# Summing modulation vectors 1024 columns at a time in a two-layer conditioned decoder trunk

## The chip, the cores and the metric

The kernel runs on one core of one Trainium2 chip. The metric is the device time of one execution in microseconds (us), from launch to end on that core, as the median of several runs. Engines are named PE (TensorE matmul), PEld (TensorE weight load), DVE (VectorE), ACT (ScalarE), POOL (GpSimd) and SP (the queue that issues the DMAs); SPq marks an issue on it.

## What is computed

Two layers act on 256 tokens of width 1024, all in f32. A condition vector c of 1024 numbers makes six modulation vectors of 1024 a layer, which shift, scale and gate the two sub-layers:

```python
mod = jax.nn.silu(c) @ w_ada + b_ada                       # w_ada: 1024 x 6144 a layer, 25 MB
sh1, sc1, gt1, sh2, sc2, gt2 = jnp.split(mod, 6, axis=-1)
h = adaln(rms_norm(x, g_mix), sh1, sc1)                     # h * (1 + sc1) + sh1
q_a, k_a, v_a, q_b, k_b, v_b, gate_a, gate_b = jnp.split(h @ w_in, IN_OFFSETS, axis=-1)
q_a = rope(rms_norm(q_a, qn_swa), positions)                # and k_a, q_b, k_b
mixed = sigmoid(gate_a) * (swa_attention(...) @ w_o_swa) + sigmoid(gate_b) * (moba_attention(...) @ w_o_moba)
x = x + gt1 * (mixed @ w_out)
h = adaln(rms_norm(x, g_mlp), sh2, sc2)
x = x + gt2 * (square(relu(h @ w_up)) @ w_down)
```

`rope` turns each head's two halves: `x1*cos - x2*sin` and `x2*cos + x1*sin`. With the head gains g taken in, the kernel needs one table of `g*cos` and one of `g*sin` with the halves of g swapped and the first one negated.

## The kernel before

**Matmuls in three terms.** Each f32 weight is split into a rounded high part and the rest: ACT casts 1024 columns (L440), DVE subtracts (L446), and TensorE makes three matmuls of each product (`mm3`, L522 to L524, and `mm3f`, L527 to L529). The weights come as pieces of 1 MB (`Stream`), three raw buffers deep, and each piece is split in two halves into a handful of slots that come free as TensorE has used them.

**Stages.** `lead` is the first projection, with an order written out by hand (`tc.manual_schedule`). Then `mixing(0)` (the rest of the projections, head norm and rotation, attention in eight pairs of heads, 16 gate products, the two output products), `mlp(0)`, `mixing(1)` and `mlp(1)`. Between two sub-layers stands a boundary: DVE takes the four finished accumulators times the gate vector into x (`residual`: L640, then L641), ACT sums squares (L541), POOL raises to the power -1/2 (L545), DVE scales (L552), TensorE turns the rows (L570), and ACT and DVE apply scale and shift.

**The background.** While the stages run, `tick()` is called after every few matmuls. A tick may split one more weight half, takes one step of each chain in `bg` (head norm, rotation, attention), and one step of the first generator in `slow` (two while `pace` is 2, which holds in the last part of `mixing(0)`). The generators in `slow` are `ada_unit(u)`. What is left of them when an output product ends is run to its end there (L661).

**A unit before.** A unit is 512 columns of one of the six vectors. Row p*8+k of `w_ada` lies on partition p, so `silu(c) @ w_ada` is a sum of eight rows on each partition and then a sum over partitions. The unit loads four pieces of two rows by 512 columns (512 KB, L233; three buffers `araw`), takes eight DVE steps, one for each row (L256 for the first of a shift or scale, else L259), one a tick, into one of two `ada` buffers, and then has a tail. For a shift or scale the tail is four TensorE turns (L288), a DVE reduction (L294) and small DVE steps (L301, L304). For a gate it is a cast on ACT (L270), a subtraction on DVE (L271), two matmuls with ones (L274, L275), and a copy on ACT (L277). A gate's first step adds the bias row, which stands in row 0 of `bz` (memset on POOL at L150, loaded at L240). Steps to a unit: 13 for a gate, 11 for a shift or scale. Units 0 to 3 belong to the lead. `ADA_PLAN` gives units 4 to 9 to `mixing(0)`, 10 to 19 to `mlp(0)`, 20 and 21 to `mixing(1)`, 22 and 23 to `mlp(1)`.

**What sets the order.** Outside the lead a planner orders each engine's instructions with a list schedule: among those that its own costs show as ready, the one that stands first in the program is issued. So a later instruction can run early where an engine would be idle, and it holds the engine until it is done. At run time every engine, and SP's queue, keeps that order and waits at its head.

**Rotary tables.** `rope_gains` (called in the lead, L1036) scales the head gains by 8 and makes the swapped copy `gsw`; `rope_tables(l)` makes the tables of a layer in eight DVE steps (L383), in the lead for layer 0 (L1021).

Of the kernel before, what the change touches and what calls it, by code (L numbers as in the profile page):

```python
# [8 lines left out]
F32 = mybir.dt.float32  # L9
# [6 lines left out]
P = 128  # L16
S = 256
D = 1024
# [55 lines left out]
ADA_PLAN = (range(4, 10), range(10, 20), range(20, 22), range(22, 24))  # L74
# [4 lines left out]
def kernel(ctx: ExitStack, tc: tile.TileContext, io):  # L79
# [39 lines left out]
    gsw = const.tile([P, DEPTH, 4, HD], F32, name="gsw")  # L119
# [29 lines left out]
    bz = const.tile([P, 512], F32, name="bz")  # L149
# [47 lines left out]
    for l in range(DEPTH):  # L197

        if l == 0:
            ada_units += [(0, 0, q) for q in range(4)]  # L200
        for parts in (((2,), (4, 3), (5,)) if l == 0 else ((1, 0), (4, 3), (2,), (5,))):
            for half in range(2):
                for part in parts:
                    ada_units.append((l, part, half))
# [5 lines left out]
    def ada_load(i):  # L210

        u, q = divmod(i, 4)
# [3 lines left out]
        col = part * D + half * 512  # L216
# [10 lines left out]
        if u < 4:  # L227
            for k in range(2):
                nc.sync.dma_start(
                    ada_raw[i][:, k, :].rearrange("p (a c) -> p a c", a=2),  # L230
                    src[:, 2 * q + k, 0:2 * D].rearrange("p (a c) -> p a c", a=2)[:, :, half * 256:half * 256 + 256])
        else:
            nc.sync.dma_start(ada_raw[i], src[:, 2 * q:2 * q + 2, col:col + 512])  # L233

    def bias_row(u):

        if u < len(ada_units) and ada_units[u][1] % 3 == 2:
            l, part, half = ada_units[u]
            c0 = part * D + half * 512
            nc.sync.dma_start(bz[0:1, :], io["b_ada"][l:l + 1, c0:c0 + 512])  # L240

    def ada_unit(u):

        l, part, half = ada_units[u]
        sub, kind = divmod(part, 3)
        acc = work.tile([P, 512], F32, tag="ada", name=nm("ada"), bufs=2)
        for q in range(4):
            for a in range(ADA_BUFS if u > 3 else 0):
                ada_load(4 * u + q + a)
            raw = ada_raw[4 * u + q]  # L250
            if q == 2:
                bias_row(u + 1)
            for k in range(2):
                kk = 2 * q + k
                if kk == 0 and kind < 2:
                    nc.vector.tensor_scalar(out=acc, in0=raw[:, k, :], scalar1=cs[:, kk:kk + 1], scalar2=None,  # L256
                                            op0=ALU.mult)
                else:
                    nc.vector.scalar_tensor_tensor(  # L259
                        out=acc, in0=raw[:, k, :], scalar=cs[:, kk:kk + 1], in1=(bz if kk == 0 else acc),  # L260
                        op0=ALU.mult, op1=ALU.add)
                yield
        yield
        if kind == 2:
            ps = tmp_t()
            if half == 0:
                gt[l][sub] = state.tile([P, D], F32, tag="gt", name=nm("gt"), bufs=2)
            hi = ring(512, "ghi").bitcast(F32R)
            lo = ring(512, "glo").bitcast(F32R)
            nc.scalar.copy(hi, acc)  # L270
            nc.vector.tensor_tensor(out=lo, in0=acc, in1=hi.bitcast(F32), op=ALU.subtract)  # L271
            for _ in range(G_LAG):
                yield
            nc.tensor.matmul(ps, lhsT=ones_r, rhs=hi, start=True, stop=False)  # L274
            nc.tensor.matmul(ps, lhsT=ones_r, rhs=lo, start=False, stop=True)  # L275
            yield
            nc.scalar.activation(gt[l][sub][:, half * 512:(half + 1) * 512], ps, AF.Copy,  # L277
                                 scale=(0.5 if sub == 0 else 1.0))
        else:
            ps = ada_sums(acc)  # L280
            yield
            ada_columns(l, sub, half, ps, 4, (kind,))
# [84 lines left out]
    def rope_gains():  # L367

        r8 = float(HD) ** 0.5
        nc.vector.tensor_scalar(out=gsw[:, :, :, 0:HALF], in0=gqk[:, :, :, HALF:], scalar1=-r8, scalar2=None,  # L370
                                op0=ALU.mult)
        nc.vector.tensor_scalar(out=gsw[:, :, :, HALF:], in0=gqk[:, :, :, 0:HALF], scalar1=r8, scalar2=None,
                                op0=ALU.mult)
        nc.vector.tensor_scalar(out=gqk, in0=gqk, scalar1=r8, scalar2=None, op0=ALU.mult)

    def rope_tables(l):

        ct = state.tile([P, 4, NT, HD], F32, tag="ct", name=nm("ct"), bufs=1)
        st = state.tile([P, 4, NT, HD], F32, tag="st", name=nm("st"), bufs=1)
        for t in range(NT):  # L380
            for h in range(2):
                for (o, g, i) in ((ct, gqk, 1), (st, gsw, 0)):
                    nc.vector.tensor_tensor(  # L383
                        out=o[:, :, t, h * HALF:(h + 1) * HALF], in0=g[:, l, :, h * HALF:(h + 1) * HALF],
                        in1=sincos[:, i, t, :][:, None, :].to_broadcast([P, 4, HALF]), op=ALU.mult)
# [495 lines left out]
    def lead():  # L881
# [113 lines left out]
        for q in range(4):  # L995
# [39 lines left out]
            if q == 0:  # L1035
                rope_gains()  # L1036
                load_rest()
# [235 lines left out]
```

## Time and profile before

| | |
|---|---|
| device time, 3 runs | 757.29 us median, 754.62 to 758.05 |
| the profiled execution: device time, span | 755.65 us, 753.9 us |
| PE busy | 730.7 us (97%), 4713 matmuls |
| PEld busy | 645.3 us (86%) |
| DVE busy | 587.2 us (78%), 1090 instructions |
| ACT busy | 431.2 us (57%) |
| POOL busy | 32.0 us (4%) |
| DMA | 173.46 MB, 230 GB/s over the span |
| TensorE's granted clock | 1.000 in the mean, full in all 40 slices |

The profiled execution lies 1.75 us outside its span, and 1.64 us under the median. Matmuls overlap and their ends are modelled, so a busy PE can hide small gaps; where PE is shown idle, it waited.

### The profile page before, as it was taken

How to read it: one execution, taken by the hardware profiler on the slowest of the kernel's cores; microseconds unless marked ns; L12 is line 12 of the kernel's file. 1: busy time of each engine (PE TensorE's matmuls, PEld its weight loads, DVE VectorE, ACT ScalarE, POOL GpSimd, SP SyncE). 2: the span in 40 equal slices, each digit the busy share in tenths (PEclk: the TensorE clock that was granted, in tenths of full speed). 3: DMA queues.
4: the chain of work that ended last, by engine and by line, in shares of the span. 5: the costliest groups of instructions: out<-in, count | busy, mean ns of one | idle time of the engine just before them, and what ended most of it. 6: DMA issues, size and time to landing. Idle time of an engine off the chain costs nothing.

```text
span 753.9 us, 12320 instructions
## 1 busy us (share of the span) xinstructions
PE 730.7 (97%) x4713; PEld 645.3 (86%) x4713; DVE 587.2 (78%) x1090; ACT 431.2 (57%) x817; POOL 32.0 (4%) x24
## 2 busy tenths in 40 slices
PE   7999889999999999999999999999999999999997
PEld 6678778899778999989977888989988899999896
DVE  6598998999899988988789788987879745545542
ACT  6545579863466655455436357576447755555550
POOL 1003200000000000000000401000000000000000
PEclk9999999999999999999999999999999999999999
DMA  8996758877949999989882633844662865565501
GB/s 293 392 325 227 227 162 285 274 254 248 303 128 330 370 347 299 332 309 342 283 318 98 224 119 113 263 157 166 225 223 80 269 203 175 182 207 172 189 33 57
DMA packets 110538, 173.46 MB, mean 230 GB/s; under 512 B 4744, under 2 KB 68488, under 8 KB 110480
## 3 DMA queue, kind: packets, MB, share of 16 engines
q1 hardware_dynamic: 109744, 172.54, 67.9%
q8 instruction: 37, 0.61, 0.3%
q10 hardware_dynamic: 736, 0.15, 0.1%
q14 instruction: 21, 0.17, 0.1%
HBM read 171.62 MB, written 1.05 MB: 229 GB/s over the span
## 4 chain that ended last, share of the span: by engine, by line
PE 72%; DVE 13%; DMA 7%; ACT 3%; issue 2%; POOL 2%; SPq 0%; ACTq 0%; DVEq 0%; POOLq 0%
PE tmp L527 11%; PE acc L524 11%; PE acc L522 11%; PE acc L523 11%; PE tmp L528 10%; PE tmp L529 10%; DMA araw<-in_w_ada_dram 4%; DVE ada L259 2%; DVE w L446 2%; PE acc L984 2%; POOL rs L751 1%; ACT w L440 1%; PE tmp L870 1%; DMA wraw<-in_w_up_dram 1%; PE acc L810 1%
## 5 line engine op out<-in xcount | busy, mean ns | idle before, releaser
L446 DVE TENSOR_TENSOR w<-wraw,w 128x1024 fp32r<-128x1024 f32 x137 | 166.3, 1221 | 48.1 <-ACT w L440 46.8
L440 ACT CAST w<-wraw 128x1024 fp32r<-128x1024 f32 x150 | 155.9, 1048 | 78.9 <-PE acc L524 44.5
L527 PE MATMUL tmp<-hT_hi,w 128*128 128x256 f32 x480 | 140.1, 292 | 1.3 <-DVE alo L874 1.2
L529 PE MATMUL tmp<-hT_hi,w 128*128 128x256 f32 x480 | 135.9, 283 | 0.0
L528 PE MATMUL tmp<-hT_lo,w 128*128 128x256 f32 x480 | 135.7, 283 | 0.0
L259 DVE SCALAR_TENSOR_TENSOR ada<-araw,cs,ada 128x512 f32<-128x512 f32 x140 | 104.4, 746 | 3.2 <-DMA araw<-in_w_ada_dram 2.1
L527 PEld LDWEIGHTS tmp<-hT_hi,w 128*128 128x128 f32 x480 | 91.5, 191 | 8.2 <-issue 4.4
L528 PEld LDWEIGHTS tmp<-hT_lo,w 128*128 128x128 f32 x480 | 91.7, 191 | 0.7
L529 PEld LDWEIGHTS tmp<-hT_hi,w 128*128 128x128 f32 x480 | 91.6, 191 | 0.3 <-issue 0.3
L522 PE MATMUL acc<-w,uhi 128*128 128x512 f32 x192 | 75.4, 393 | 0.0
L523 PE MATMUL acc<-w,uhi 128*128 128x512 f32 x192 | 74.9, 390 | 0.0
L524 PE MATMUL acc<-w,ulo 128*128 128x512 f32 x192 | 74.9, 390 | 0.0
L1164 ACT ACTIVATE relu<-tmp 128x256 f32<-128x256 f32 x56 | 21.5, 384 | 68.8 <-PE tmp L529 68.8
L524 PEld LDWEIGHTS acc<-w,ulo 128*128 128x128 f32 x192 | 36.1, 188 | 7.6
L522 PEld LDWEIGHTS acc<-w,uhi 128*128 128x128 f32 x192 | 36.1, 188 | 6.9
L523 PEld LDWEIGHTS acc<-w,uhi 128*128 128x128 f32 x192 | 36.1, 188 | 6.8
L440 ACT CAST kv<-wraw 128x1024 fp32r<-128x1024 f32 x21 | 22.1, 1051 | 24.6 <-PE acc L524 19.8
L446 DVE TENSOR_TENSOR ahi<-wraw,ahi 128x1024 fp32r<-128x1024 f32 x18 | 22.0, 1222 | 15.0 <-ACT ahi L440 14.9
L446 DVE TENSOR_TENSOR kv<-wraw,kv 128x1024 fp32r<-128x1024 f32 x21 | 25.7, 1222 | 9.9 <-ACT kv L440 9.8
L446 DVE TENSOR_TENSOR qT<-wraw,qT 128x1024 fp32r<-128x1024 f32 x21 | 25.6, 1220 | 8.3 <-ACT qT L440 8.3
L527 PE MATMUL tmp<-hT_hi,alo 128*128 128x256 f32 x112 | 31.8, 284 | 0.0
L528 PE MATMUL tmp<-hT_lo,alo 128*128 128x256 f32 x112 | 31.7, 283 | 0.0
(248 smaller groups left out, 1744.8 us busy)
## 6 DMA issues: line engine op xcount, KB each, us to landing
araw<-in_w_ada_dram SPq DMA_DIRECT2D x80, 512.0 KB, 5.9
wraw<-in_w_up_dram SPq DMA_DIRECT2D x32, 1024.0 KB, 5.9
wraw<-in_w_down_dram SPq DMA_DIRECT2D x32, 1024.0 KB, 5.9
wraw<-in_w_in_dram SPq DMA_DIRECT2D x28, 1024.0 KB, 5.7
wraw<-in_w_out_dram SPq DMA_DIRECT2D x8, 1024.0 KB, 5.6
wraw<-in_w_in_dram SPq DMA_DIRECT2D x12, 512.0 KB, 7.1
wraw<-in_w_o_swa_dram SPq DMA_DIRECT2D x8, 512.0 KB, 3.3
wraw<-in_w_o_moba_dram SPq DMA_DIRECT2D x8, 512.0 KB, 5.1
```

The costliest lines, as they stand in the source:

```text
L259: nc.vector.scalar_tensor_tensor(out=acc, in0=raw[:, k, :], scalar=cs[:, kk:kk + 1], in1=(bz if kk == 0 else acc), op0=ALU.mult, op1=ALU.add)
L440: nc.scalar.copy(hi, r)
L446: ins = nc.vector.tensor_tensor(out=lo, in0=r, in1=hi.bitcast(F32), op=ALU.subtract)
L522: nc.tensor.matmul(ps, lhsT=lh, rhs=rh, start=start, stop=False)
L523: nc.tensor.matmul(ps, lhsT=lh, rhs=rl, start=False, stop=False)
L524: nc.tensor.matmul(ps, lhsT=ll, rhs=rh, start=False, stop=stop)
L527: nc.tensor.matmul(ps, lhsT=wh, rhs=ah, start=start, stop=False)
L528: nc.tensor.matmul(ps, lhsT=wh, rhs=al, start=False, stop=False)
L529: nc.tensor.matmul(ps, lhsT=wl, rhs=ah, start=False, stop=stop)
L751: nc.gpsimd.tensor_tensor(out=rs, in0=ss, in1=mhalf[:, :NT * nh].rearrange("p (t h) -> p t h", h=nh), op=ALU.pow)
L984: T.matmul(ps[t], lhsT=left[:, 2 * q + k, t * P:(t + 1) * P], rhs=w[:, k, :], start=(first and k == 0), stop=(last and k == 1))
L1164: nc.scalar.activation(r, ps, AF.Relu)
```

## The change

Units 4 and up become whole vectors of 1024 columns, one row of `w_ada` a piece (still 512 KB). There are 10 of them in place of 20, with one `ada` buffer of 1024 in place of two of 512. The order of the vectors in layer 1 and the share of each stage stay as they were. Both halves of the tail run one after the other at the end of the unit. In `mixing(0)`'s shift and scale (units 5 and 6) the tail is the lead's `columns` (four matmuls with one column of ones, L335) instead of turns and a reduction. `rope_gains` and `gsw` go; `rope_tables` takes the unscaled gains with swapped halves and the factor 8 or -8 as a scalar.

```diff
-ADA_PLAN = (range(4, 10), range(10, 20), range(20, 22), range(22, 24))
+ADA_PLAN = (range(4, 7), range(7, 12), range(12, 13), range(13, 14))
...
-    bz = const.tile([P, 512], F32, name="bz")
+    bz = const.tile([P, D], F32, name="bz")
...
-            nc.sync.dma_start(ada_raw[i], src[:, 2 * q:2 * q + 2, col:col + 512])
+            nc.sync.dma_start(ada_raw[i].rearrange("p k c -> p (k c)"), src[:, q, part * D:(part + 1) * D])
...
-        acc = work.tile([P, 512], F32, tag="ada", name=nm("ada"), bufs=2)
+        acc = work.tile([P, D], F32, tag="ada", name=nm("ada"), bufs=1)
+        for k in range(KT):
+            for a in range(ADA_BUFS):
+                ada_load(16 + 8 * (u - 4) + k + a)
+            raw = ada_raw[16 + 8 * (u - 4) + k].rearrange("p k c -> p (k c)")
+            if k == 4:
+                bias_row(u + 1)
+            if k == 0 and kind < 2:
+                nc.vector.tensor_scalar(out=acc, in0=raw, scalar1=cs[:, k:k + 1], scalar2=None, op0=ALU.mult)
+            else:
+                nc.vector.scalar_tensor_tensor(out=acc, in0=raw, scalar=cs[:, k:k + 1], in1=(bz if k == 0 else acc),
+                                               op0=ALU.mult, op1=ALU.add)
+            yield
         yield
+        for half in range(2):
+            hs = slice(half * 512, (half + 1) * 512)
+            if kind == 2:
...
+                nc.scalar.copy(hi, acc[:, hs])
+                nc.vector.tensor_tensor(out=lo, in0=acc[:, hs], in1=hi.bitcast(F32), op=ALU.subtract)
+                for _ in range(G_LAG):
+                    yield
...
+            elif u in ADA_PLAN[0]:
+                ps = columns(acc[:, hs])
+                yield
+                ada_affine(l, sub, half, ps, 4, (kind,))
+            else:
+                ps = ada_sums(acc[:, hs])
+                yield
+                ada_columns(l, sub, half, ps, 4, (kind,))
...
-                for (o, g, i) in ((ct, gqk, 1), (st, gsw, 0)):
-                    nc.vector.tensor_tensor(
-                        out=o[:, :, t, h * HALF:(h + 1) * HALF], in0=g[:, l, :, h * HALF:(h + 1) * HALF],
+                for (o, i, f, gh) in ((ct, 1, r8, h), (st, 0, (r8 if h else -r8), 1 - h)):
+                    nc.vector.scalar_tensor_tensor(
+                        out=o[:, :, t, h * HALF:(h + 1) * HALF], in0=gqk[:, l, :, gh * HALF:(gh + 1) * HALF], scalar=f,
...
-                rope_gains()
                 load_rest()
```

## Rows read from the trace of the kernel before

**Rows 1.** Stretch: length; busy us (count) PE, PEld, DVE, ACT, POOL; clock, DMA, GB/s.
```profile
0.00:58.00 58.00, 51.77 (x279) 40.75 (x280) 41.16 (x92) 30.99 (x48) 2.81 (x10) 1.00 0.95 332
58.00:105.00 47.00, 40.75 (x263) 34.48 (x262) 42.03 (x94) 25.53 (x51) 12.48 (x4) 1.00 0.60 198
105.00:205.00 100.00, 98.80 (x740) 89.02 (x739) 92.03 (x205) 68.33 (x166) 0.00 (x0) 1.00 0.82 269
205.00:225.00 20.00, 17.53 (x96) 14.28 (x95) 19.44 (x42) 12.89 (x27) 1.61 (x2) 1.00 0.46 147
225.00:389.00 164.00, 164.00 (x1048) 149.23 (x1047) 143.45 (x201) 91.42 (x148) 0.00 (x0) 1.00 0.95 327
389.00:405.00 16.00, 13.37 (x66) 10.50 (x65) 14.17 (x32) 6.08 (x17) 1.47 (x2) 1.00 0.48 174
405.00:754.00 349.00, 344.50 (x2233) 306.99 (x2231) 234.97 (x431) 195.99 (x366) 13.61 (x6) 1.00 0.51 168
```

**Rows 2.** What PE waited for: us in total, times, longest.
```profile
PE tmp L570 <- DVE ln L552: 4.1, 2, 2.4
PE acc L984 <- ACT hT_hi L970: 3.2, 2, 2.0
```

**Rows 3.** The tile `ada`: instructions, ns min/median/max, first to last start in us, shapes.
```profile
L259 DVE SCALAR_TENSOR_TENSOR ada<-araw,cs,ada x140: 722/746/754, 75.5 to 499.1; 128x512 f32<-128x512 f32 x140
...
L256 DVE TENSOR_SCALAR ada<-araw,cs x12: 475/480/486, 119.0 to 350.2; 128x512 f32<-128x512 f32 x12
L259 DVE SCALAR_TENSOR_TENSOR ada<-araw,cs,bz x8: 740/746/752, 62.5 to 485.6; 128x512 f32<-128x512 f32 x8
```

**Rows 4.** DVE's groups by line: count, busy us, mean ns, idle before and its cause.
```profile
L446 DVE TENSOR_TENSOR w<-wraw,w 128x1024 fp32r<-128x1024 f32 x137 | 166.3, 1221 | 48.1 <-ACT w L440 46.8 <-PE tmp L793 0.7
...
L294 DVE TENSOR_REDUCE cols<-tmp 128x4 f32<-128x512 f32 x12 | 8.2, 686 | 2.5 <-PE tmp L288 2.5
```

**Rows 5.** Order of time, boundary before `mixing(1)`: start, us, instruction [idle before <- cause].
```profile
390.90 1.53 DVE L259 SCALAR_TENSOR_TENSOR ada<-araw,cs,ada 128x512 f32<-128x512 f32 x2
392.36 0.68 DVE L640 TENSOR_TENSOR res<-acc,gt 128x512 f32<-128x512 f32 x1
392.96 0.74 DVE L259 SCALAR_TENSOR_TENSOR ada<-araw,cs,ada 128x512 f32<-128x512 f32 x1
393.62 0.68 DVE L641 TENSOR_TENSOR x_sb<-x_sb,res 128x512 f32<-128x512 f32 x1
394.22 0.74 DVE L259 SCALAR_TENSOR_TENSOR ada<-araw,cs,ada 128x512 f32<-128x512 f32 x1
...
397.27 0.66 PE L570 MATMUL tmp<-cpack,ln 128*128 128x128 f32 x4 [2.43 <-DVE ln L552]
```

**Rows 6.** The lead's rotary tables and `columns`: ns min/median/max, first to last start.
```profile
L383 DVE TENSOR_TENSOR ct<-gqk,sincos x8: 262/283/286, 37.8 to 144.1; 128x128 f32<-128x128 f32 x8
...
L335 PE MATMUL tmp<-ones,arow x16: 169/250/250, 27.8 to 40.1; 128*128 128x1 f32 x16
```

**Rows 7.** Tile `ada` alone by stretch: busy us (count) PE, PEld, DVE, ACT.
```profile
58.00:105.00 47.00, 0.00 (x0) 0.00 (x0) 8.10 (x11) 0.64 (x1) 1.00 0.60 198
105.00:205.00 100.00, 2.39 (x16) 1.88 (x16) 29.69 (x42) 0.65 (x1) 1.00 0.82 269
...
225.00:389.00 164.00, 4.79 (x32) 3.83 (x32) 60.76 (x85) 1.22 (x2) 1.00 0.95 327
```

**Rows 8.** Order of time during `mixing(0)`'s rotation.
```profile
75.52 0.74 DVE L259 SCALAR_TENSOR_TENSOR ada<-araw,cs,ada 128x512 f32<-128x512 f32 x1
...
77.01 0.63 PE L793 MATMUL tmp<-cpack,ro 128*128 128x128 f32 x4 [1.09 <-DVE ro L785]
```

**Rows 9.** Order of time on DVE: unit 6's reduction, then unit 8's first step.
```profile
151.49 0.69 DVE L294 TENSOR_REDUCE cols<-tmp 128x4 f32<-128x512 f32 x1 [1.09 <-PE tmp L288]
152.09 0.48 DVE L256 TENSOR_SCALAR ada<-araw,cs 128x512 f32<-128x512 f32 x1
```

**Rows 10.** POOL's power at the boundaries: ns min/median/max, first to last start.
```profile
L545 POOL TENSOR_TENSOR lnr<-lnr,mhalf x6: 557/668/938, 206.0 to 570.5; 128x1 f32<-128x1 f32 x6
```

More of the change, by code (lines that the diff above doesn't have):

```diff
@@ L200 @@
             ada_units += [(0, 0, q) for q in range(4)]
[L201 to L204, printed above, removed]
+        ada_units += [(l, part, None) for part in ((2, 4, 3, 5) if l == 0 else (1, 0, 4, 3, 2, 5))]
     ada_raw = {}
@@ L232, in ada_load @@
         else:
-            nc.sync.dma_start(ada_raw[i], src[:, 2 * q:2 * q + 2, col:col + 512])
+            nc.sync.dma_start(ada_raw[i].rearrange("p k c -> p (k c)"), src[:, q, part * D:(part + 1) * D])
     def bias_row(u):
         if u < len(ada_units) and ada_units[u][1] % 3 == 2:
-            l, part, half = ada_units[u]
-            c0 = part * D + half * 512
-            nc.sync.dma_start(bz[0:1, :], io["b_ada"][l:l + 1, c0:c0 + 512])
+            l, part, _ = ada_units[u]
+            nc.sync.dma_start(bz[0:1, :], io["b_ada"][l:l + 1, part * D:(part + 1) * D])
@@ L242, in ada_unit @@
     def ada_unit(u):
-        l, part, half = ada_units[u]
+        l, part, _ = ada_units[u]
         sub, kind = divmod(part, 3)
-        acc = work.tile([P, 512], F32, tag="ada", name=nm("ada"), bufs=2)
[L247 to L251, printed above, removed]
-                bias_row(u + 1)
[L253 to L262, printed above, removed]
+        acc = work.tile([P, D], F32, tag="ada", name=nm("ada"), bufs=1)
@@ L263, in ada_unit @@
         yield
         if kind == 2:
[L265 to L272, printed above, removed]
-                yield
-            nc.tensor.matmul(ps, lhsT=ones_r, rhs=hi, start=True, stop=False)
@@ L275, in ada_unit @@
[L275 to L282, printed above, removed]
+            gt[l][sub] = state.tile([P, D], F32, tag="gt", name=nm("gt"), bufs=2)
+        for half in range(2):
+            hs = slice(half * 512, (half + 1) * 512)
+            if kind == 2:
+                ps = tmp_t()
+                hi = ring(512, "ghi").bitcast(F32R)
+                lo = ring(512, "glo").bitcast(F32R)
+                nc.scalar.copy(hi, acc[:, hs])
+                nc.vector.tensor_tensor(out=lo, in0=acc[:, hs], in1=hi.bitcast(F32), op=ALU.subtract)
+                for _ in range(G_LAG):
+                    yield
+                nc.tensor.matmul(ps, lhsT=ones_r, rhs=hi, start=True, stop=False)
+                nc.tensor.matmul(ps, lhsT=ones_r, rhs=lo, start=False, stop=True)
+                yield
+                nc.scalar.activation(gt[l][sub][:, hs], ps, AF.Copy, scale=(0.5 if sub == 0 else 1.0))
+            elif u in ADA_PLAN[0]:
[6 more added lines that the diff above has]
+                ada_columns(l, sub, half, ps, 4, (kind,))
@@ L365, in rope_sin @@
         nc.scalar.activation(pos_f, pos_f, AF.Tanh)
[L367 to L374, printed above, removed]
     def rope_tables(l):
@@ L379, in rope_tables @@
         st = state.tile([P, 4, NT, HD], F32, tag="st", name=nm("st"), bufs=1)
+        r8 = float(HD) ** 0.5
         for t in range(NT):
             for h in range(2):
-                for (o, g, i) in ((ct, gqk, 1), (st, gsw, 0)):
-                    nc.vector.tensor_tensor(
-                        out=o[:, :, t, h * HALF:(h + 1) * HALF], in0=g[:, l, :, h * HALF:(h + 1) * HALF],
-                        in1=sincos[:, i, t, :][:, None, :].to_broadcast([P, 4, HALF]), op=ALU.mult)
+                for (o, i, f, gh) in ((ct, 1, r8, h), (st, 0, (r8 if h else -r8), 1 - h)):
+                    nc.vector.scalar_tensor_tensor(
+                        out=o[:, :, t, h * HALF:(h + 1) * HALF], in0=gqk[:, l, :, gh * HALF:(gh + 1) * HALF], scalar=f,
+                        in1=sincos[:, i, t, :][:, None, :].to_broadcast([P, 4, HALF]), op0=ALU.mult, op1=ALU.mult)
         return ct, st
```

4 lines of the change are left out of this document (1 added, 3 removed).

## The prediction, made before the change was run

> **What bounds the kernel now.** I read the engines by stretch first [rows 1]. In the 754 us of the span the reader is to look at PE's busy time against the length. From 225 to 389 us, which is `mlp(0)`, PE is busy 164.00 of 164, at the full clock. From 405 to the end it lacks 4.5 of 349 us, nearly all at the very end. PE's idle time adds up to 23 us and lies in few places: 6.2 us in the first 58 us (the lead), 6.25 us from 58 to 105 (rotation and first attention pairs of `mixing(0)`), 1.2 us from 105 to 205, and 2.5 and 2.6 us in the two boundaries at 205 and 389. Whatever the change does for another engine, only these places can give time back, and the lead and the end are hardly touched. The list of PE's waits names the two boundaries: 4.1 us in two waits for the scaling step L552 on DVE, the longer one 2.4 [rows 2].
>
> DVE is the second engine, and where PE has its gaps DVE is nearly full: 42.0 of 47 us from 58 to 105, and 19.4 of 20 at the first boundary [rows 1]. The order of time shows why that counts. At the second boundary four accumulating steps stand between the residual steps. Two hold DVE from 390.90 to 392.36, so the next L640 starts only then. The third puts L641 off by 0.66, the fourth L640 by 0.66. That is 2.78 us of background work in one chain, and at its end PE has waited 2.43 us [rows 5]. At 205 the same picture has three such steps and the other 1.7 us of the 4.1. In the rotation a step at 75.52 stands in front of the rotated rows for which PE waits 1.09 us [rows 8].
>
> **The steps and their price.** Before, 148 steps of 0.746 and 12 of 0.48 make 116.2 us on DVE [rows 3]. After, there are 10 units of eight: 74 accumulating steps of 1024 and six plain ones. The trace has no accumulating step of 1024. It has a two-input step at 512 (0.68, L640 [rows 5]) and at 1024 (1.221, L446 [rows 4]), so 512 more columns cost 0.54, and I estimate 0.746 + 0.54 = 1.29. Bounds: 1.22 like L446, and 1.49 for two old steps. A plain one costs 0.48 to 0.96, I take 0.75. Sum 74 x 1.29 + 6 x 0.75 = 100 us, so 16 us less (6 more to 22 less). Four reductions go as well, 4 x 0.686 = 2.7 us [rows 4]. None of this is time of the kernel by itself, since PE is the bound; its price is worked out by place below.
>
> **Lead, +0.5 us.** Eight table steps become steps of the accumulating kind. In the order of time a step of that kind holds DVE 0.66, a two-input one of the same width 0.60 [rows 5], so each costs 0.06 more, eight 0.5. They stand on DVE at 37.8 us and after [rows 6], ahead of the shift and scale of the next quarter, and for those PE waits through ACT's L970 (3.2 us in two waits [rows 2]), so I charge it in full. Ends: 0, if that wait has another cause, and 0.9. The three steps of `rope_gains` go, but I give nothing for them: they stand a stage earlier, where DVE waits for the next weights; without that cover they would be worth three steps like L383's 0.28 [rows 6] or a little wider, 1 us. The larger memset of `bz` is hidden too: POOL is busy 2.8 us in the first 58 [rows 1]; at worst it costs 0.5.
>
> **58 to 205 us, +2.0 us.** The ticks are the same and a tick still takes one step, but a step is now 1024 wide. Before, unit 4 took its eight steps in the eight ticks of the last projection, and unit 5 began after its tail. Now unit 4 puts eight steps of 1.29 and both subtractions before 105: 8 x 1.29 + 2 x 0.68 = 11.7 us, where the trace has 8.1 in 11 instructions [rows 7]. That is 3.6 us more on a DVE that has 5 us free there. Later it turns: units 4 to 6 take 31 us in all, those of before 37.8 up to 205 (8.10 + 29.69 [rows 7]), and the reductions go. But from 105 to 205 PE lacks only 1.2 us, so the relief comes where it buys little. Ends: -1.0, if that gap goes and the early work finds free places, and +4.3, eight longer steps of 0.54 each on PE's path. PE can take gate products in between as long as their weights are split ahead, so I stay near the middle, a little above. The four `columns` matmuls and four turns cost PE the same: 0.25 each at most [rows 6] against 2.39 / 16 = 0.15 [rows 7], 16 of them, under 2 us either way in a stretch where they fill between others; I take 0.
>
> **First boundary, -0.8 us.** A unit's first step can't run before the tail of the unit that had its buffer: unit 8's first step starts 0.6 us after unit 6's reduction [rows 9]. With one buffer, unit 7 follows unit 6's tail, well before 205, and its eight steps fill the idle places of DVE that units 8 and 9 leave. If all eight are done by 200, the boundary has none and the 1.7 us come back. I expect one to three to be left, which are longer now. Ends: -1.7 and +1.6 (three at 0.54 more).
>
> **`mlp(0)`, 0 us.** By steps the background would run faster: 8 of 12 steps of a unit are sums of 1.29 (0.86 us a tick), before 8 of 11 at 0.746 (0.54). 1.59 times the 60.8 us of [rows 7] would ask DVE for 143 + 36 = 179 us in 164. It can't get that: the DMA is 0.95 busy at 327 GB/s, and the most in [rows 1] is 332, so the pieces come little faster than before through three buffers. Each piece is now free after one step, so SP issues the next sooner, with the weights' loads behind it in the same queue. Weight halves are split several ahead, which hides a few us. Ends: 0 and +5, a third of the excess of 15 us; the third is a choice.
>
> **Second boundary, -2.2 us.** From `mixing(0)`'s end to here are six whole vectors, the same 48 pieces as before, but they start up to 40 us earlier. Unit 12 then has its sum done before 389, and unit 13 can't start: its buffer waits for unit 12's tail, which stands in `mixing(1)`. So the four steps go from the boundary. Next late is L640 itself, which waits for PE, so not all 2.43 come back. Ends: -2.4 and 0 (two steps of 1.29 for four of 0.7).
>
> **A rule weighed.** POOL's power, one number a row, took 0.557 to 0.938 us [rows 10]; the cause of that spread is not in the rows, and 0.38 is the most it can cost. The Trainium skill (SBUF — State Buffer, Who interferes with whom) says that a VectorE instruction with two SBUF inputs and a GpSimd instruction that reads SBUF exclude each other for the whole of the one that started first. By that rule a power behind a sum of 1024 would wait up to 0.54 us longer at each boundary, and the sum below would be +0.6 instead of -0.5. By the row I take nothing, as I expect few sums there.
>
> **Sum.** 0.5 + 2.0 - 0.8 + 0 - 2.2 = -0.5 us. `mixing(1)` and `mlp(1)` get one unit each where PE has no gap: 0. Against the profiled execution (753.9 of span and 1.75 around it, 755.65) this gives 755.15; that execution lies 1.64 under the median of 757.29, so I forecast 756.8: no change that can be told. A measurement here tells about 0.5%, 3.8 us, from no change.
>
> **Rivals.**
> Slower, by the length of the step in the way: DVE takes a step when it is idle and holds it to the end, so each critical step that comes just after waits 1.29 where it waited 0.75. Price: lead 0.5, rotation 4.3, first boundary 1.6, second -2.2 = +4.2, 761.5 (763.7 if the second boundary keeps its steps). For it: DVE's 42 of 47 us and the wait behind 75.52. Against it: half as many steps. It decides once PE's idle time from 58 to 105 passes some 10 us.
> Faster, by cleared boundaries: both lose their steps and the rotation finds room. 0.5 - 1.0 - 1.7 - 2.4 = -4.6, 752.7. For it: rows 5; against it: the DVE load before 105.
> Slower in `mlp(0)`, by pieces that DVE waits for in order while weight halves stand behind: 0.5 + 2.0 - 0.8 - 2.2 + 5 = +4.5, 761.8. For it: a DMA at 0.95; against it: no PE gap in 164 us so far.
>
> **Chances.** Forecast 0.50, step in the way 0.17, boundaries cleared 0.23, `mlp(0)` 0.10. From 751.5 to 762.5 the forecast's own spread, most of the faster case and a good half of the slower ones are held. Faster by over 0.5%: 0.19 of the second rival and 0.05 of the forecast's tail, 0.24. Slower: 0.13 + 0.08 + 0.04 = 0.25. The rest, 0.51, is within.
>
> **What would show it.** Accumulating steps of 1024 at 1.22 to 1.49 us, DVE near 568 us in all. No such step between the residual steps at the second boundary, and a wait for L552 there under 0.5 us; at the first one at most three. PE's idle time from 58 to 105 near 8 us, and later in the lead by half a us. `mlp(0)` without a PE gap, its background done before 380. I am wrong if PE waits in `mlp(0)`, if the second boundary keeps its steps, or if the rotation moves by more than 4 us either way.

## The result and the profile after

The changed kernel takes 767.64 us in the median of six runs (766.06 to 769.64), the kernel before 756.89 in the median of six (754.62 to 758.99): ratio 1.0143, 95% interval 1.0119 to 1.0168. It is slower by 10.8 us, where 756.8 was forecast and 762.5 was the end of the range. The profiled execution takes 768.69 us with a span of 766.9, which is 13.0 more than the span shown of before.

DVE did what was worked out. These are the steps of the background from the view of the tile `ada` after (instructions, ns min/median/max, first to last start; they answer to [rows 3]):

```profile
L250 DVE SCALAR_TENSOR_TENSOR ada<-araw,cs,ada x70: 1273/1278/1286, 78.4 to 505.9; 128x1024 f32<-128x1024 f32 x70
...
L248 DVE TENSOR_SCALAR ada<-araw,cs x6: 744/746/747, 112.8 to 310.2; 128x1024 f32<-128x1024 f32 x6
```

A step takes 1.28 us (1.29 was the estimate), DVE as a whole 573.4 us against 587.2 (568 was forecast). So the work fell by 14 us and the time rose by 13. To see where, I cut both spans at three marks that every variant has, each at its start: the first square of head norm (end of the lead), the last L627 of the first boundary, and the last L627 of the second (L640 before). The four stretches are called lead, mixing(0), mlp(0) and rest here. Windows of before (columns as in [rows 1]):

```profile
0.00:56.75 56.75, 50.52 (x273) 39.73 (x274) 40.54 (x91) 29.75 (x46) 2.81 (x10) 1.00 0.95 336
56.75:209.29 152.54, 142.96 (x1017) 125.91 (x1015) 138.51 (x308) 97.42 (x223) 13.42 (x5) 1.00 0.75 245
209.29:398.81 189.52, 186.75 (x1164) 168.00 (x1164) 167.99 (x249) 105.06 (x176) 1.54 (x2) 1.00 0.89 308
398.81:753.90 355.09, 350.49 (x2263) 311.62 (x2261) 240.19 (x445) 199.01 (x374) 14.20 (x7) 1.00 0.50 165
```

Windows of after, the same four stretches and then five short ones:

```profile
0.00:59.56 59.56, 53.69 (x273) 42.53 (x274) 39.87 (x88) 29.78 (x46) 3.35 (x10) 0.91 0.90 312
59.56:217.13 157.57, 149.34 (x1033) 131.58 (x1031) 140.14 (x284) 97.28 (x222) 14.08 (x5) 0.97 0.78 263
217.13:412.34 195.21, 189.51 (x1168) 169.32 (x1166) 154.62 (x199) 105.83 (x178) 1.22 (x2) 0.99 0.81 281
412.34:766.90 354.56, 349.81 (x2260) 311.18 (x2258) 238.74 (x436) 198.38 (x373) 14.20 (x7) 1.00 0.50 165
...
80.00:84.00 4.00, 2.22 (x12) 1.70 (x13) 4.00 (x6) 1.17 (x2) 1.20 (x1) 0.87 0.70 200
84.00:88.00 4.00, 4.00 (x19) 3.32 (x18) 4.00 (x9) 0.65 (x1) 0.00 (x0) 0.71 0.87 289
100.00:104.00 4.00, 1.46 (x11) 1.26 (x10) 1.44 (x5) 1.95 (x3) 2.53 (x1) 0.93 0.92 311
104.00:108.00 4.00, 4.00 (x19) 3.35 (x18) 4.00 (x15) 1.86 (x8) 0.00 (x0) 0.50 0.22 79
328.00:332.00 4.00, 3.94 (x14) 3.10 (x14) 2.80 (x4) 0.00 (x0) 0.00 (x0) 0.59 0.86 282
```

The reader is to see two things. The 13.0 us are +2.8 in the lead, +5.0 in mixing(0) with the first boundary, +5.7 in mlp(0) with the second, and -0.5 in the rest. And the column of the granted clock, which was 1.00 in every row of before, is not any more: it fell to half, 1.2 of 2.4 GHz, in places. PE's busy time in mixing(0) rose by 6.4 us while its idle time fell from 9.6 to 8.2.

What PE waited for after (us in total, times, longest), answering to [rows 2]:

```profile
PE tmp L780 <- DVE ro L772: 2.7, 2, 1.7
PE acc L509 <- ACT w L427: 2.7, 1, 2.7
PE tmp L283 <- DVE ada L250: 2.7, 1, 2.7
PE acc L797 <- DVE qn L745: 2.5, 1, 2.5
...
PE tmp L557 <- DVE ln L539: 0.4, 1, 0.4
```

The boundary waits are gone as forecast: 0.4 us in one wait where 4.1 stood. Two waits that before had not at all took their place, L509 and L283; the wait of L797, in the rotation, grew from 1.2 to 2.5 us. L509 and L283 lie in mlp(0), and the order of time shows how each comes about, after one place of the rotation (start, us, instruction [idle before <- cause]):

```profile
78.45 1.28 DVE L250 SCALAR_TENSOR_TENSOR ada<-araw,cs,ada 128x1024 f32<-128x1024 f32 x1
79.64 0.69 DVE L772 TENSOR_TENSOR ro<-ra,rb 128x512 f32<-128x512 f32 x1
80.48 0.30 PE L780 MATMUL tmp<-cpack,ro 128*128 128x128 f32 x1 [1.65 <-DVE ro L772]
...
283.17 1.22 DVE L433 TENSOR_TENSOR kv<-wraw,kv 128x1024 fp32r<-128x1024 f32 x1
284.30 1.28 DVE L250 SCALAR_TENSOR_TENSOR ada<-araw,cs,ada 128x1024 f32<-128x1024 f32 x1
285.73 0.63 PE L283 MATMUL tmp<-cpack,ada 128*128 128x128 f32 x4 [2.66 <-DVE ada L250]
...
313.62 4.19 SPq L228 DMA_DIRECT2D araw<-in_w_ada_dram  x3
317.90 0.39 SPq L405 DMA_DIRECT2D wraw<-in_w_down_dram  x1
...
323.46 0.39 PE L509 MATMUL acc<-kv,uhi 128*128 128x512 f32 x1
...
325.91 2.00 ACT L427 CAST w<-wraw 128x1024 fp32r<-128x1024 f32 x2 [4.49 <-DMA wraw<-in_w_down_dram]
327.01 1.20 PE L509 MATMUL acc<-w,uhi 128*128 128x512 f32 x4 [2.71 <-ACT w L427]
...
329.37 0.63 PE L511 MATMUL acc<-w,ulo 128*128 128x512 f32 x1
```

At 78.45 a step stands ahead of the rotated rows, and PE waits 1.65 us ([rows 8] showed 1.09 at the same place). At 285.73 PE's order holds the turns of a sum whose last step is not done; everything behind them waits too. At 327.01 the weights themselves are late: ACT has waited 4.49 us for a piece of `w_down`. SP issued that piece at 317.90, behind three loads of `w_ada` that held its queue from 313.62 on. Behind the wait the clock is 0.59, and a product that took 0.39 us takes 0.63.

### The profile page after: what moved, and what is told of

Its sections match the earlier page's. It is cut to its first block, busy times and chain, and to the rows that moved or that the text cites. A ratio compares the mean times of both kernels' runs of the same rounds, so it can differ in the third digit from the quotient of the medians.

```text
span 766.9 us, 12257 instructions
## 1 busy us (share of the span) xinstructions
PE 742.4 (97%) x4729; PEld 654.6 (85%) x4729; DVE 573.4 (75%) x1003; ACT 431.3 (56%) x817; POOL 32.9 (4%) x24
## 4 chain that ended last, share of the span: by engine, by line
PE 78%; DVE 11%; DMA 5%; issue 2%; POOL 2%; ACT 2%; ACTq 0%; DVEq 0%; POOLq 0%; SPq 0%
PE tmp L514 11%; PE tmp L516 11%; PE tmp L515 11%; PE acc L510 11%; PE acc L511 11%; PE acc L509 10%; DMA araw<-in_w_ada_dram 3%; PE acc L971 3%; DVE ada L250 2%; DVE w L433 2%; POOL rs L738 2%; PE acc L797 2%; PE tmp L857 2%; PE tmp L841 1%; DMA wraw<-in_w_down_dram 1%
## 5 line engine op out<-in xcount | busy, mean ns | idle before, releaser
L250 DVE SCALAR_TENSOR_TENSOR ada<-araw,cs,ada 128x1024 f32<-128x1024 f32 x70 | 89.6, 1279 | 9.0 <-DMA araw<-in_w_ada_dram 8.8
L509 PE MATMUL acc<-w,uhi 128*128 128x512 f32 x192 | 75.0, 393 | 2.7 <-ACT w L427 2.7
L509 PEld LDWEIGHTS acc<-w,uhi 128*128 128x128 f32 x192 | 36.0, 188 | 9.9 <-ACT w L427 3.1
L427 ACT CAST qT<-wraw 128x1024 fp32r<-128x1024 f32 x21 | 22.1, 1052 | 21.4 <-PE acc L511 6.0
```

The source lines that it names most:

```text
L250: nc.vector.scalar_tensor_tensor(out=acc, in0=raw, scalar=cs[:, k:k + 1], in1=(bz if k == 0 else acc), op0=ALU.mult, op1=ALU.add)
L427: nc.scalar.copy(hi, r)
L509: nc.tensor.matmul(ps, lhsT=lh, rhs=rh, start=start, stop=False)
```

## Experiments

Two questions had to be kept apart: which of the two edits costs the time, and by what way the wide sums cost it. Each experiment was timed beside the kernel before on the same chip, where that kernel's median lay between 756.6 and 758.0 us; the ratio is to that kernel, with its 95% interval. This table has the time of each with its four stretches, worked out from windows of its profile as above (PE's clock in brackets where it isn't 1.00). The expectations that name a time of mlp(0) count it without the second boundary, up to the first residual step: 180.3 us before, 185.9 after.

| kernel | median, us | ratio | lead | mixing(0) | mlp(0) | rest |
|---|---|---|---|---|---|---|
| before | 756.9 | 1 | 56.8 | 152.5 | 189.5 | 355.1 |
| after | 767.6 | 1.0143 [1.0119, 1.0168] | 59.6 (.91) | 157.6 (.97) | 195.2 (.99) | 354.6 |
| rope_alone | 756.3 | 0.999 [0.996, 1.002] | 59.0 (.91) | 151.4 (.99) | 187.5 | 356.8 |
| sums_alone | 769.2 | 1.014 [1.009, 1.019] | 56.7 | 156.1 (.98) | 197.5 (.97) | 356.0 |
| spread | 761.4 | 1.004 [1.002, 1.007] | 56.6 (.97) | 156.8 (.97) | 189.5 | 355.5 |
| halves_spread | 762.8 | 1.005 [1.002, 1.008] | 57.5 (.97) | 159.8 (.96) | 190.1 | 355.3 |
| before_dense | 770.1 | 1.017 [1.012, 1.021] | 56.3 (.97) | 157.6 (.97) | 199.7 (.98) | 355.6 |
| halves_dense | 762.5 | 1.006 [1.004, 1.009] | 59.3 (.91) | 156.5 (.98) | 190.6 | 355.2 |
| spread_mlp | 759.7 | 1.004 [1.001, 1.006] | 57.8 (.94) | 157.3 (.97) | 187.6 | 355.1 |
| late | 760.7 | 1.004 [1.001, 1.006] | 58.2 (.94) | 151.8 (.99) | 190.8 | 355.1 |
| noload | 758.0 | 1.001 [0.998, 1.004] | 58.5 (.94) | 157.6 (.97) | 187.2 | 354.5 |
| poolq | 779.1 | 1.031 [1.024, 1.037] | 56.8 (.97) | 159.1 (.97) | 207.1 (.96) | 354.6 |
| late2 | 765.6 | 1.013 [1.004, 1.022] | 59.3 (.91) | 159.2 (.97) | 193.8 (.99) | 355.1 |
| lead_awake | 756.7 | 1.001 [0.998, 1.004] | 59.8 (.94) | 153.4 (.99) | 188.4 (.99) | 355.3 |
| noload_all | 757.5 | 1.000 [0.998, 1.002] | 62.8 (.92) | 153.2 (.98) | 187.3 | 354.5 |
| halfload | 762.6 | 1.006 [1.004, 1.008] | 59.3 (.91) | 157.7 (.97) | 191.0 (.99) | 354.3 |
| spread_mlp_tail | 758.8 | 1.000 [0.998, 1.002] | 56.9 | 154.0 (.98) | 187.8 | 355.0 |
| tail_only | 758.2 | 1.001 [0.999, 1.003] | 57.6 (.94) | 155.6 (.97) | 189.0 | 354.8 |
| late_tail | 763.7 | 1.008 [1.005, 1.011] | 59.5 (.91) | 154.8 (.98) | 191.2 | 355.1 |
| ease | 773.0 | 1.020 [1.016, 1.023] | 57.7 (.97) | 170.0 (.95) | 189.8 | 355.8 |

One profile stands behind each row of stretches. Runs of the kernel before differ by 8 us and those of late2 by 11, so a stretch is read with the median beside it.

**The two edits apart.** rope_alone puts the diff's rotary part alone into the kernel before. sums_alone is the changed kernel with the swapped copy back; as the wide sums leave no room for it, it lies in a ring buffer:

```diff
+            gsw_of[l] = ring(4 * HD, "gsw")...
+                for (o, g, i) in ((ct, gqk, 1), (st, gsw, 0)):
```

> The kernel before with only the rotary tables made from gqk with scalar_tensor_tensor, no swapped copy. Theory A (the loss comes from the wide sums; the lead's 2.8 us are a clock that fell by chance of phase): within 1 us of before, 756 to 758 us. Theory B (the rotary edit delays the lead and through it all that follows): 759 to 761 us, with the first square of the lead near 59.5 us against 56.75.

> The changed kernel with the rotary tables made as before from swapped gains (kept in a ring buffer, layer 1's swap made just ahead of its tables). Theory A (wide sums are the loss): 765 to 770 us, like the changed kernel. Theory B (rotary edit costs the lead): 763 to 765 us, 2.8 us less than the changed kernel.

Measured 0.999 and 1.014: the rotary edit is worth nothing that can be told, and the sums are the loss. Theory B falls by its times. The 2.8 us of the lead are no part that the medians show: rope_alone has the same slow lead (59.0 at a clock of .91) at an unchanged median, and sums_alone a quick one (56.7) at a median as slow as after. One thing stays open: 15 of the 16 profiles with the rotary edit have a clock of .97 or less in the lead, and of the three with the old tables and no dummies one has. Whether the edit makes that fall more frequent was not tried.

**Half the pace.** spread gives each step two ticks, halves_spread cuts each step into two of 512 columns, one a tick:

```diff
             yield
+            yield
```

> The changed kernel with one more yield after each 1024-column step, so that a unit takes as many ticks as its two halves did before and the DVE work and DMA bytes per tick are those of before; the step stays 1.28 us wide. Theory A1 (density: twice the work per tick crowds the rotation and mlp(0)): 755 to 759 us, PE waits in the rotation under 1.3 us each and no wait of 2.7 us in mlp(0). Theory A2 (width: a 1.28 us step ahead of a short one is the harm, however seldom): 763 us or more.

> The changed kernel with its 1024-column loads, but each step cut into two of 512 columns, one per tick: density and width of before, loads and units of after. Theories A1 and A2 both: 755 to 760 us. If it stays above 764 us, neither step width nor density is the cause, and the loads of one row (or the single sum buffer and the later turns) are.

Both get back half of the loss or more, 761.4 and 762.8, and do not differ clearly: at this pace no effect of a step's width is seen. mlp(0) is back at 189.5 and 190.1. But neither reaches 760, and both miss their forecasts. In the profiles mixing(0) keeps its loss, 156.8 and 159.8, and halves_spread has there both the pace and the width of before. So half the pace does not give mixing(0) back, and what costs it is open.

**The pace in the old kernel, and the width at the new one.** before_dense takes two old steps a tick; halves_dense takes the wide step as two narrow ones in the same tick:

```diff
-        for _ in range(2 if clock[0] % 2 < pace[0] else 1):
+        for _ in range(4 if clock[0] % 2 < pace[0] else 2):
```

> The kernel before, unchanged but for its tick: two (four where it took two) of its 512-column steps are taken per tick, which is the pace of bytes and of DVE work of the changed kernel. Theory A1 (density is most of the loss): 762 to 767 us, with PE waits over 2 us in the rotation or in mlp(0) as in the changed kernel. Theory A3 (the loads of one row, the single sum buffer or the later turns are the loss): 756 to 759 us.

> The changed kernel with each 1024-column step cut into two of 512 columns in the same tick: density of the changed kernel, width of before. Theory A1 (density): 765 to 770 us. Theory A2 (width): 760 to 763 us, as with the halves spread over two ticks (762.8).

The pace alone, with nothing else of the change, makes the old kernel at least as slow as the changed one: 770.1, above the 767 that A1 had as its end, its mlp(0) 199.7. halves_dense goes by A2 and not by A1, at 762.5: at the dense pace the width does count, 5 us of it, and mostly in mlp(0) (190.6 against 195.2). By what way it counts there is not shown. So pace and width act together, which neither theory had said.

**Which stage.** spread_mlp keeps mixing(0) dense and gives the extra tick to all later units.

```diff
             yield
+            if u not in ADA_PLAN[0]:
+                yield
```

> The changed kernel with the extra tick per step everywhere but in the first mixing stage: its three units there stay dense. By the profiles mlp(0) is 6 to 8 us of the loss and the rotation with the first gates 3 to 5. If the two add up: 761 to 764 us. If the loss of mlp(0) follows from what the mixing stage left late: 766 us or more. If mlp(0) is all of it: 759 to 761 us, not above the kernel with the extra tick everywhere (761.4).

759.7, not above spread: the pace in mlp(0) is what the extra ticks repair. ACT's waits for weights between 236 and 336 us show how (us in total, times, longest). After:

```profile
ACT w L427 <- DMA wraw<-in_w_down_dram: 8.8, 3, 4.5
ACT w L427 <- DMA wraw<-in_w_up_dram: 6.4, 3, 4.2
ACT qT L427 <- DMA wraw<-in_w_down_dram: 5.7, 1, 5.7
ACT ahi L427 <- DMA wraw<-in_w_up_dram: 3.0, 2, 2.8
```

spread_mlp, where this is all that ACT waits for a transfer:

```profile
ACT w L429 <- DMA wraw<-in_w_down_dram: 0.5, 1, 0.5
```

And this is what was transferred in 100 us of mlp(0), first before from 228 us, then after and spread_mlp from 236 (loads, KB each, median us to landing):

```profile
DMA packets 19190, 33.41 MB, mean 334 GB/s; under 512 B 704, under 2 KB 10235, under 8 KB 19182
...
araw<-in_w_ada_dram SPq DMA_DIRECT2D x26, 512.0 KB, 6.7
wraw<-in_w_down_dram SPq DMA_DIRECT2D x10, 1024.0 KB, 7.0
wraw<-in_w_up_dram SPq DMA_DIRECT2D x9, 1024.0 KB, 7.0
```

```profile
DMA packets 14189, 32.28 MB, mean 323 GB/s; under 512 B 736, under 2 KB 8186, under 8 KB 14182
...
araw<-in_w_ada_dram SPq DMA_DIRECT2D x31, 512.0 KB, 5.8
wraw<-in_w_up_dram SPq DMA_DIRECT2D x8, 1024.0 KB, 8.0
wraw<-in_w_down_dram SPq DMA_DIRECT2D x7, 1024.0 KB, 7.9
```

```profile
DMA packets 15027, 30.63 MB, mean 306 GB/s; under 512 B 656, under 2 KB 9872, under 8 KB 15019
...
araw<-in_w_ada_dram SPq DMA_DIRECT2D x24, 512.0 KB, 6.8
wraw<-in_w_up_dram SPq DMA_DIRECT2D x10, 1024.0 KB, 7.9
wraw<-in_w_down_dram SPq DMA_DIRECT2D x9, 1024.0 KB, 7.0
```

The transfers run nearly as fast as before (323 against 334 GB/s), and what changed is whose they are: after has 31 pieces of the sums and 15 of the weights, the two others 26 and 24 pieces and 19 of the weights. SP issues in the order of the program, and with a piece taken in each tick more of them stand ahead of each load of weights. That these late weights are what costs PE its time is not shown by this; the turns below speak to it.

**No loads, half the loads, another queue.** noload lets the steps of mlp(0)'s units read the piece that lies in the buffer already, noload_all does so in mixing(0) too, halfload for every second piece; in these three the sums concerned are of wrong rows. poolq has the pieces of mlp(0) issued by GpSimd's queue.

```diff
+        if 7 <= u < 12:          # noload_all: 4 <= u < 12; halfload: 7 <= u < 12 and q % 2
+            ada_raw[i] = ada_raw[i - ADA_BUFS]
+            return
```
```diff
-            nc.sync.dma_start(...)
+            (nc.gpsimd if 7 <= u < 12 else nc.sync).dma_start(...)
```

> The changed kernel, dense, but the five units of mlp(0) load nothing: each step reads the piece that lies in its buffer already, so their sums are of wrong rows. All its DVE steps, turns and waits on buffers stay. Theory M1 (mlp(0) loses by its loads: pieces arrive late, and SP's queue holds weight loads behind them): mlp(0) falls from 186 to 188 us to 178 to 181, the time to 758 to 762 us. Theory M2 (DVE steps and unit ends put in front of TensorE's inputs): mlp(0) stays at 185 or more, the time at 765 to 769 us.

> The changed kernel, dense, with the loads of mlp(0)'s five units issued by GpSimd's queue in place of SyncE's: the same bytes, but no weight load stands behind a load that waits for its buffer. Theory M1a (the queue order on SP is the harm): mlp(0) 178 to 182 us, time 758 to 762 us. Theory M1b (bytes per us: the loads themselves come late): mlp(0) 184 us or more, time 765 to 769 us.

> As the kernel whose mlp(0) loads none of its five units, and the three units of the first mixing stage load nothing either (all these sums are of wrong rows); steps, turns and waits stay. Theory X1 (the mixing stage loses to DVE steps ahead of the rotary work): rotation to the end of the first boundary stays at 156 to 158 us against 152.6 before, the time at 757 to 759 us as without loads in mlp(0) alone. Theory X2 (loads crowd the mixing stage as well): 152 to 154 us there, 753 to 755 us in all.

> The changed kernel, dense, with every second piece of mlp(0)'s units not loaded (its step reads an older one, so these sums are of wrong rows): the bytes per tick are those of before, the DVE steps dense and 1.28 us wide. Theory R (rate: what the pieces take of the transfers beyond what was left is missing in the weights): 757 to 760 us, mlp(0) at 178 to 181 us. Theory L (each load that waits for its buffer holds what stands behind it): about half the loss of mlp(0) stays, 761 to 764 us.

noload is at 758.0 with every step and every turn as dense as after: without the loads mlp(0) loses nothing (M1), and M2 falls. Its window of mlp(0):

```profile
216.14:403.39 187.25, 187.05 (x1168) 168.28 (x1166) 153.88 (x198) 105.72 (x178) 1.22 (x2) 1.00 0.63 211
```

187.25 is 2.3 less than before, which is the gain that the cleared second boundary had been given.

poolq missed both of its forecasts. With the weights no longer behind the pieces, PE does not wait for weights at all, but 14.0 us for three sums:

```profile
PE tmp L283 <- DVE ada L250: 14.0, 3, 6.3
```

DVE waits 19.4 us for pieces there, where after has 7.9. So the order of SP's queue decides who is late: with it the weights and the sums a little, without it the sums a lot. halfload lies between (762.6, mlp(0) 191.0), the number of theory L; but what is left there is no weight that waits, it is one wait of 2.1 us for a unit's last sum, with the clock at 0.58 behind it. I count it as undecided between R and L, and as a pointer to the turns.

noload_all brings mixing(0) to 153.2, as X2 said, but not the time of X2 (757.5), and it is no clean test: with no piece to wait for, four of its first unit's steps went into the lead (5.1 us of DVE there, where after has none), and the lead took 62.8. Between X1 and X2 it leaves open.

**The turns.** Both kernels below put three ticks more between a unit's last step and the turns of its sum; tail_only changes nothing else of the changed kernel.

```diff
-        yield
+        for _ in range(1 + TAIL):      # TAIL = 3
+            yield
```

> As the kernel with the extra tick per step outside the first mixing stage, with three ticks more between a unit's last step and the turns of its sum. If turns planned too early cost the remaining 0.37%: 755 to 758 us. If they cost nothing here: 759 to 761 us, as without.

> The changed kernel, dense, with only three ticks more between a unit's last step and the turns of its sum. If turns planned too early are a large part of the loss (2.7 us in mlp(0) and half clock): 761 to 764 us. If the late weights are nearly all of it: 765 to 769 us, and waits for the casts of late weights stay in mlp(0).

tail_only missed: 758.2 where 761 at the least was expected. Nine of the 10.8 us come back with 15 more ticks in mlp(0), nine in mixing(0), and no load taken away; by the profiles 6.2 of them in mlp(0) and 2.0 in mixing(0). Between 236 and 336 us it moves 31 pieces and 16 of weights, hardly other than after. What it no longer has is a wait of PE for weights; of the waits in mlp(0) behind its start this one is left, and then its window:

```profile
PE tmp L285 <- DVE ada L251: 1.6, 1, 1.6
```

```profile
213.21:402.19 188.98, 187.09 (x1165) 168.59 (x1166) 156.01 (x199) 106.09 (x180) 1.22 (x2) 1.00 0.84 295
```

spread_mlp_tail has both repairs and the ratio 1.000 (758.8, between its two forecasts). So the loss of mlp(0) needs two things at once: loads at the dense pace, so that pieces and weights come just in time or a little late, and an order without slack, in which PE stands behind a sum that is a tick from done. Taking away all the loads, half the pace or the lack of slack is each enough, or nearly (187.3, 187.6 and 189.0); taking away half the loads is not (191.0).

Of the two late things the sums weigh more. halves_dense moves 31 pieces and 15 of weights in the same 100 us as after, and ACT waits 19.4 us for weights there against 23.9, yet PE waits for no weight in mlp(0). In tail_only, with 31 and 16 and 9.4 us of such waits on ACT, it is the same. All that PE waits for in halves_dense, but for 0.2 us, is this:

```profile
PE tmp L286 <- DVE ada L253: 2.9, 2, 2.5
```

PE waits for a sum in halfload, halves_dense, poolq and after, in sums_alone (2.4) and before_dense (4.4); it waits for a weight as well only in after, sums_alone (3.3) and before_dense (4.9).

**An emptied rotation.** late holds mixing(0)'s units back until the fifth gate product and then takes them densely; late2 starts after the second gate, one step a tick; late_tail is late with the later turns; lead_awake is the kernel before with dummy matmuls in the lead's gaps; ease takes a step every second tick up to tick 24, with the later turns. All but lead_awake have the extra tick of spread_mlp in the later stages.

```diff
+            if l == 0 and j == LATE:       # 4; late2: 1
+                slow.extend(ada_unit(u) for u in ADA_PLAN[0])
```
```diff
+            if (u not in ADA_PLAN[0] and k < KT - 2) or (u in ADA_PLAN[0] and clock[0] < EASE):
+                yield
```

> The changed kernel with the extra tick per step outside the first mixing stage, and in that stage no step before the fifth gate: then one per tick, two at the end; the last unit is done at tick 54 of 70. Theory A1 (steps in the rotation stand ahead of DVE work that TensorE waits for): rotation and first seven gates take 58 to 62 us against 62.4 before and 66 to 68 in the dense ones, and the time is 753 to 758 us. Rival (DVE is short in the output products, where the steps go instead): 760 us or more, with TensorE waits for DVE after 160 us.

> As the kernel with the late steps, but started after the second gate and one per tick throughout (the last unit ends at tick 56 of 70), the extra tick per step in the later stages. If the start at the fifth gate pushed too much into the output products (47.2 us there against 41.1, with waits of 3.2 us for the low halves of the weights): rotation to gate 6 takes 58 to 61 us, the output products 41 to 44 us, the time is 754 to 758 us. If DVE is simply full over the whole mixing stage: 759 us or more, whatever the start.

> As the kernel with the late steps in the first mixing stage (start at the fifth gate), with three ticks more between a unit's last step and the turns of its sum, so that it ends at tick 59 of 70. If the waits and half-clock stretches behind turns planned too early took the gain of the emptied rotation: 753 to 757 us, faster than before by up to 0.5%. If DVE is full in the output products: 759 to 762 us, as without.

> Steps at every second tick up to tick 24 of the first mixing stage, one or two per tick after it, the extra tick per step in the later stages, and three ticks more ahead of the turns. If the rotation then takes what it took before (30.9 us) and the output products no more (41): 753 to 756 us, faster than before by 0.2 to 0.5%. If DVE is full over the mixing stage, whatever the order: 757 to 760 us.

late shows what a step in the rotation is worth: from the first square to the seventh gate it takes 57.4 us, the kernel before 62.4. The output products give it all back, as the rival said: 47.2 us up to the first residual step against 41.1, with PE waiting for the low half of a weight:

```profile
PE acc L513 <- DVE w L436: 3.2, 1, 3.2
```

late2, late_tail and ease are worse in the median (765.6, 763.7 and 773.0), late2 with runs from 759.9 to 771.1; the two with later turns miss both of their forecasts. In late_tail and ease PE waits for a last sum in mixing(0) after all, three ticks or not (late_tail, then ease):

```profile
PE tmp L335 <- DVE ada L252: 4.8, 2, 3.5
```

```profile
PE tmp L335 <- DVE ada L252: 4.4, 1, 4.4
```

Why the ticks that clear mlp(0) do not clear these is open. No version beat both kernels; the best, spread_mlp_tail, equals the one before.

> The kernel before with three dummy 128x128 matmuls more behind each of the four turns of the lead (12 in all), which lie in its gaps. Theory C (the spread of the runs from 754 to 762 us is a clock that falls to half in the lead or behind the gaps of the rotation, by chance of a few tenths of a us): the lead's clock stays at 1.00, mean clock 0.994 to 0.998, median 754 to 756 us. Rival (the lead's clock is no part of the spread): 757 us or more at a mean clock of 0.989 to 0.995.

lead_awake is inconclusive. Its lead still had a clock of .94, so the dummies did not do what they were put in for, and the time did not change.

## Why the prediction was wrong

**mlp(0), 0 us: the step that failed.** It saw that the background would ask for more there, saw the transfers at 0.95, and concluded that "the pieces come little faster than before". They came faster, 31 in 100 us against 26, and the weights slower, 15 against 19: the full transfers did not hold back the one who asked for more, they took from the other. It also trusted weight halves that are split ahead to hide what comes late, and PE waited 2.7 us for one. And it had no term at all for the turns of a unit, which come one tick behind its last step; in an order that is fixed, that tick is all the slack there is, and PE waited 2.7 us there. Beside noload (187.25) mlp(0) with the second boundary lost 8.0 us in after, 5.5 of it in PE's idle time and 2.5 in its busy time, at a clock of .99. So the term is about +8, where 0 was put and +5 was its end. tail_only shows that the turns are the half that decides: the shift of the loads stays, and 6.2 us of mlp(0) come back. A wait of PE in mlp(0), one of the prediction's own signs of being wrong, was there. The rival for mlp(0), at 0.10, had the price of +5 and a mechanism near to this one (DVE waits for pieces, weight halves behind them); DVE's waits for pieces there grew from 3.6 to 7.9 us, but it had the turns no more than the forecast had.

**58 to 205 us, +2.0: the wait right in kind, the size wrong.** Up to the first residual step it came out at +4.2, and the first boundary at +0.8, so +5.0 in all where +1.2 had been worked out. A step in the way of the rotation was seen, and PE's wait there grew from 1.09 to 1.65. But PE's idle time in mixing(0) did not grow at all, 9.6 to 8.2 us; its busy time did, by 6.4 us. At a mean clock of 0.97, three hundredths of 157.6 us are 4.7 us. The prediction had no term for the clock: it was 1.00 in all rows of before, and I read that as a property of the kernel. It varies from one execution to the next. Of 25 later runs of the same kernel none had a mean clock over .998; the quickest had .995 (754.2 us), the slowest .989 (762.4 us). The time does not follow the clock alone: of 17 runs in the last round one had 1.000 (756.1 us) and one .999 (757.1 us). rope_alone and lead_awake, whose mixing(0) is that of before, have a fall at the same place (0.62 from 100 to 104 us, 0.70 from 108 to 112), so not all of the 4.7 us need be the change's. In the table, mixing(0) takes 151 to 155 us wherever its clock is .98 or more, with two exceptions at 156, and 156 to 160 where it is .96 or .97 with one exception at 155.6 (ease, at .95, has other waits as well). That this is cause and not only company was not tried by itself, and neither the pace nor the width of the steps is needed for the loss: halves_spread has those of before, and the longest mixing(0) but ease's.

**The boundaries, -0.8 and -2.2: right for PE's waits.** No step stands in the second boundary after, and where nothing disturbs it, in noload, mlp(0) with the second boundary is 2.3 us shorter than before. In the first one two steps are left, as one to three were expected, and the wait for L539 is 0.4 us where 1.7 stood; but from its first to its last residual step it took 9.4 us against 8.6. POOL's power, put at nothing, took 0.550 to 0.942 us after against 0.557 to 0.938.

**Lead, +0.5: right within what can be told,** by rope_alone, whose interval reaches from 2.9 us quicker to 1.4 slower. The +2.8 of the profile go with a clock of .91 there against 1.00 in the one execution shown of before.

**DVE's bounds.** "6 more to 22 less" does not come out of the prices beside it: 74 x 1.49 + 6 x 0.96 make 116.0 us, as much as before and not more. Nothing hangs on it.

**The rival "step in the way"** said that it decides once PE's idle time from 58 to 105 us passes 10; it was 7.8 (39.22 busy of 47), and mixing(0) lost 5.0 us all the same, with a lower clock. **The range** ended at the sum of one rival at a time. In size two of them, the rotation and mlp(0), came together. mlp(0)'s loss follows from the dense pace, since spread_mlp gives it back; for mixing(0) that is not shown.

## What to carry to other kernels

Work in the background has a pace as well as an amount. If a change doubles what one tick takes, try it with half the ticks that take it: here the dense loads displaced those of the foreground though the total was the same, and half the pace outside mixing(0) brought the ratio from 1.014 to 1.004. Behind a sum that another engine still has to finish, leave slack in the order before the engine that must not wait: three ticks were worth nine of 10.8 us here, with the loads as they were. And 14 us less on an engine that is not the bound made no version faster than the kernel before.

## What the runs showed of the hardware

**The clock falls behind some short waits.** In after PE waits 1.65 us at 80.48, and 1.08 once more right behind; the clock is 0.71 from 84 to 88. It waits 2.54 at 103.31, and the clock is 0.50 from 104 to 108; 2.71 at 327.01, and it is 0.59 from 328 to 332. An estimate from these three rows of four us is 1.2, 2.0 and 1.6 us lost by the clock, beside the waits. The wait of 2.66 at 285.73 had no such fall behind it, and neither had the 2.43 at the second boundary of before [rows 5]. What sets the two kinds apart is not shown. The Trainium skill (TensorE: Matmul & The Clock Gate, HAM oscillation — how this bites in real kernels) describes a kernel whose clock drops again and again behind waits for DMAs. The place at 327.01 agrees with that, a wait of 2.71 us behind a late load and then a clock of 0.59; the falls behind 80.48 and 103.31 came behind waits for DVE.

**A queue of its own for the pieces did not help here.** In poolq a piece took 5.9 us from issue to landing between 236 and 336 us (median, 5.8 in after), so it was not slower on GpSimd's queue. Yet PE lost 14.2 us of 207.1 in mlp(0) by waiting, against 5.7, with the 16 engines' share at 0.75 against 0.81. Why the sums came that late is not shown.
